# A hybrid decoder step on one Trainium2 core: the new tokens' products in two float32r passes over stacked high and low parts

## The chip, the cores and the metric

The kernel runs on one core of one Trainium2 chip. The metric is device time in microseconds (us) of one execution, as the median of several runs. The engines are named as in the profile: PE (TensorE; PEld is its weight load), DVE (VectorE), ACT (ScalarE), POOL (GpSimd) and SP (SyncE, which here issues the DMAs).

## The reference

Two trunk layers work on 512 prompt tokens and on 8 samples with 8 new tokens each (64 new tokens), 1024 model columns, all in float32. Layer 0 projects the modulated tokens onto queries, keys and values of two head groups and onto an indexer; group A attends to the top-k keys that the indexer selects (128 for a prompt query, 256 for a sample's), group B to all keys with forget gates; the samples also read paged caches. Layer 1 is a chunked gMLP. Each mixer is followed by a convolutional FFN. What matters here is this, with h the modulated tokens of a layer:

```python
hp = xp * (1 + sc1p) + sh1p
hs = xs * (1 + sc1s) + sh1s
...
qa, ka, va, qi, ki, wi, qb, kb, vb, fb = jnp.split(h @ w_in, offs, axis=-1)
...
z = jax.nn.gelu(h @ w_in, approximate=False)
u, v = jnp.split(z, 2, axis=-1)
return u, layer_norm(v, lnv_g, lnv_b)
...
mix_s = (u * mixed) @ w_out_c[j]
xs = layer_norm(ALPHA * xs + (1 + g1s) * mix_s, ln1_g[i], ln1_b[i])
```

The products that the change touches are h @ w for the columns qi, vb (512 columns each), va, ka, qa (512 each) and the gMLP's v (2048), and of these the rows of the 64 new tokens only.

## The kernel before, in words

Activations lie transposed: 8 blocks kb (or k) of 128 model columns on the partitions, 576 tokens along the free axis (512 prompt tokens, then the 64 new ones). To keep float32's precision on PE at the speed of float32r, a value x is split into a high part xh, x rounded to float32r, and a low part xl = x - xh, and so is each weight (wh, wl); a product is then three float32r matmuls, high times high, high times low, low times high. `weights` (L243 to L255) loads a block of 128x1024 raw weights into wr by SP (L250), casts it to wh on ACT (L251) and subtracts to wl on DVE or POOL (L254); wr, wh and wl have three buffers each.

Most products are written with the weights stationary. The products named above are token-major: the tokens are stationary, the weights move, and the result has tokens on the partitions. `token_unit` (L685 to L703) does it for one weight load, a unit: of n = 256 weight columns the load holds four values of k, of n = 512 two. For the four blocks of 128 prompt tokens (tb 0 to 3) it calls `mm3` for each k (L283 to L285, three float32r matmuls). For the 64 new tokens (tb 4) it runs, for each k, one matmul in full float32 (L702): stationary is xn, the unsplit new tokens (128x64), moving the raw weights wr; even k go to the PSUM rows 0 to 63 and odd k to 64 to 127, each on one half of PE's columns. `both_halves` (L715) adds the two halves later, by a copy on ACT (L717) and an add on DVE (L718). The trace shows each of these matmuls as two records, so a unit of n = 256 has eight (x8), one of n = 512 four.

Three places call it. `project` multiplies qi and vb, two blocks of four units with n = 512, from `w_ab` (L836, L868). `project_a` (L920) multiplies va, ka and qa, each in two halves of two units with n = 256, from `w_aa`: 12 units; after each token block its `between` sends out pieces of the samples' attention and of the top-k selection. `gmlp` (L548) multiplies v in eight blocks of two units with n = 256, from `w_v`: 16 units, where `lead` (L573) runs tb 2, 3 and 4 of a unit and the loop below it tb 0 and 1.

The new tokens' xn has two sources. In layer 0 `modulate` (L421 to L431) makes t = x*(1+scale)+shift on DVE for each kb, copies its last 64 columns to xn on POOL (L430), and splits t into xh and xl (`split_to`: ACT copy L760, DVE subtract L761). For later products `Norm.finish` (L117 to L162) makes xn for the whole 1024 columns on DVE and splits it. Four norms exist; three of them have a next product and make xn, and only the one ahead of the gMLP has a reader of it.

The order of the instructions on each engine comes from a scheduler, from the order of the calls, priorities and the buffers that come free, so an edit of one place moves others. The DVE's top-k of the samples (MAX8 and MATCH_REPLACE8 rounds, L1068 and L1069) stands between `project` and the rest of `project_a`; it ends in the selection mask sels (L1187 to L1190). SP's queue holds all loads in order: pages of the caches (L269, tile own), weights (L250) and modulation weights (L372).

Of the kernel before, what the change touches and what calls it, by code (L numbers as in the profile page):

```python
# [10 lines left out]
F32 = mybir.dt.float32  # L11
# [7 lines left out]
P = 128  # L19
D = 1024  # L20
KB = 8
# [38 lines left out]
class Norm:  # L60
# [56 lines left out]
    def finish(self, part):  # L117
# [19 lines left out]
        if part:  # L137
            ps = psum.tile([P, KB, NS], F32, name="tp", bufs=2)
            for kb in range(KB):
                nc.tensor.transpose(ps[:, kb], rt[:NS, 4, kb * P:(kb + 1) * P], ident[:NS, :NS])  # L140
            self.xn = xp.tile([P, KB, NS], F32, name="xn")
            t = self.xn.rearrange("p k (b q) -> p k b q", b=8)
            wide = lambda m: m[:, :, :, None].to_broadcast([P, KB, 8, 8])
            nc.vector.tensor_tensor(t, ps.rearrange("p k (b q) -> p k b q", b=8), wide(self.gains), op=OP.mult)
            nc.scalar.copy(x[:, :, NP:], ps)
            nc.vector.tensor_tensor(t, t, wide(self.offs), op=OP.add)
            net.split_to(*(w[:, :, NP:] for w in self.out), self.xn)
        for k0 in range(0, KB, 2):
# [12 lines left out]
            nc.scalar.copy(h, t)  # L161
            nc.vector.tensor_sub(l, t, h.bitcast(F32))  # L162
# [40 lines left out]
class Net:  # L203
# [217 lines left out]
    def modulate(self, xk, sc1, sh, kb, pool):  # L421
# [7 lines left out]
        nc.vector.tensor_tensor(ts, ts, sh[:, kb, 1:9, None].to_broadcast([P, 8, 8]), op=OP.add)  # L429
        nc.gpsimd.tensor_copy(self.xn[:, kb], t[:, NP:])  # L430
        self.split_to(*(x[:, kb] for x in self.xhl), t)  # L431


# [114 lines left out]
    def gmlp(self, x, last, psum, pool, xp, *norm):  # L548

        nc, a, xs, xn = self.nc, self.a, last.xs, last.xn  # L550
        g1 = self.plus_one(1, 2, xp, "g1")
# [21 lines left out]
        def lead():  # L573
# [4 lines left out]
            units.append(self.weights(a["w_v"][c, u], 1024))  # L578
            self.token_unit({tb: accs[tb // 4][:, tb % 2] for tb in (2, 3, 4)}, units[u], u, 256, xs, xn, True, (2, 3, 4))

# [3 lines left out]
        for c in range(8):  # L584
            first = None
            for u in range(2):
                if c not in led or u == len(led[c][0]):
                    lead()
                units, accs = led[c]
                first = first or psum.tile([P, 2, 256], F32, name="acc", bufs=4)  # L590
                self.token_unit([first[:, 0], first[:, 1]], units[u], u, 256, xs, xn, True, (0, 1))
            accs = [first] + led.pop(c)[1]
# [91 lines left out]

    def token_unit(self, accs, w, u, n, xs, xn, shared=False, tbs=range(5), between=None):  # L685

# [4 lines left out]
        for tb in tbs:  # L691
            for j in range(per):
# [7 lines left out]
                else:  # L700
                    c = 64 * (k % 2)
                    self.nc.tensor.matmul(accs[tb][c:c + NS], xn[:, k], wk[2], start=k < 2, stop=k >= KB - 2,  # L702
                                          tile_position=(0, c))  # L703
            if between:
                between()

    def token_product(self, accs, srcs, xs, xn, n, between=None, shared=False, before=None):

        for u, src in enumerate(srcs):
            w = self.weights(src, 1024)  # L710
            if before:
                before(u)
            self.token_unit(accs, w, u, n, xs, xn, shared, between=between)

# [55 lines left out]
    def project(self, keep, pool, room, psum, free):  # L770
# [5 lines left out]
        xs = self.xs = [self.halves(tuple(x[:, kb] for x in self.xhl)) for kb in range(KB)]  # L776
        self.xn = pool.tile([P, KB, NS], F32, name="xn")
        self.sc1 = pool.tile([P, KB, 9], F32, name="sc1")
# [56 lines left out]
        toks = self.five(psum)  # L835
        self.token_product(toks, [a["w_ab"][0, u] for u in range(4)], xs, self.xn, 512, None, False, before)  # L836
        qit = self.pair(tmp, [P, 4, NP], "qit")
# [5 lines left out]
        kd = tmp.tile([P, 5, P], F32, name="kd")  # L843
        rt = tmp.tile([P, 5, 64], F32, name="rt8")
        for n, t0, t1 in ((P, 0, 4), (NS, 4, 5)):
# [18 lines left out]
        for ci, name in enumerate(("qi", "vb")):  # L864
            accs = toks
            if ci:
                accs = self.five(psum)
                self.token_product(accs, [a["w_ab"][ci, u] for u in range(4)], xs, self.xn, 512, between)  # L868
            for tb in range(5):
# [50 lines left out]
    def project_a(self, pool, psum, xs, between):  # L920
# [3 lines left out]
        for c, name in enumerate(("va", "ka", "qa")):  # L924
            for half in range(2):
                cols = slice(256 * half, 256 * half + 256)
                accs = [psum.tile([P, 2, 256], F32, name="s", bufs=5) for _ in range(3)]
                self.token_product([accs[tb // 2][:, tb % 2] for tb in range(5)], [a["w_aa"][c, half, u] for u in range(2)],
                                   xs, self.xn, 256, between, True)
                for i in range(3):  # L930
# [703 lines left out]
```

## Time and profile before

| what | value |
|---|---|
| median of 3 runs | 1940.66 us (1937.17 to 1941.69) |
| profiled execution | 1944.53 us, of which the span of its instructions is 1942.8 us |
| granted clock of PE, mean | 0.972 |
| PE busy | 1826.5 us, 94% |
| PEld busy | 1622.8 us, 84% |
| DVE busy | 1157.8 us, 60% |
| ACT busy | 743.7 us, 38% |
| POOL busy | 351.3 us, 18% |

The profile is of one execution. Busy is the time in which an engine works on an instruction; PE's matmuls are pipelined, so a matmul's length is longer than the step to the next one's start, and the step is what counts. A granted clock of 1.00 is 2.4 GHz, 0.5 is 1.2 GHz. In a row, `tc<-wr,xn` is the output's name and the inputs' names; `[4.54 <-DVE mx L1332]` is the time in which the engine sat idle before the row, and what ended it.

### The profile page before, as it was taken

Reading aid. Unit: us, or ns where it says so; the run is one execution under the profiler, and the core shown is the slowest. Engines: PE = TensorE matmul, PEld = TensorE weight load, DVE = VectorE, ACT = ScalarE, POOL = GpSimd, SP = SyncE. Lnnn points to the kernel's source line nnn. Section 1 sums busy time; section 2 is a strip of 40 time slices with the busy share of each in tenths; the row PEclk is TensorE's granted clock in tenths of the full one; section 3 lists DMA queues with packets and bytes.
Section 4 is the critical chain, followed back from the end, with each engine's and each line's share of the span. In section 5 each row is a group of like instructions: output and inputs, shape, how many; then the busy total and the mean of one; then the engine's idle time right before and its main releaser. Section 6 shows DMA issues by size and latency. Waiting matters only on the chain. (4 is left out here: it accounts for less than half of the span.)

```text
span 1942.8 us, 37068 instructions
## 1 busy us (share of the span) xinstructions
PE 1826.5 (94%) x14460; PEld 1622.8 (84%) x14460; DVE 1157.8 (60%) x2426; ACT 743.7 (38%) x1382; POOL 351.3 (18%) x518
## 2 busy tenths in 40 slices
PE   6889999899889899999999999999998999999996
PEld 4647877655459799999999989999997999999995
DVE  2549963465448754545556963465577655555577
ACT  2323222255443542424345432422234535344543
POOL 2323511110015310101012330110013101010124
PEclk9989999999899999999999999999998999999997
DMA  8346577797874335353543422332132222213242
GB/s 288 127 155 219 179 253 244 241 307 232 266 240 149 116 131 189 135 161 135 195 141 107 131 92 78 97 97 59 63 112 72 78 97 67 97 56 108 87 139 92
DMA packets 140865, 283.36 MB, mean 146 GB/s; under 512 B 32722, under 2 KB 43922, under 8 KB 140690
## 3 DMA queue, kind: packets, MB, share of 16 engines
q1 hardware_dynamic: 139970, 278.64, 43.9%
q0 software_dynamic: 720, 2.36, 0.5%
q8 instruction: 114, 1.87, 0.4%
q14 instruction: 61, 0.50, 0.1%
HBM read 270.00 MB, written 10.94 MB: 145 GB/s over the span
## 5 line engine op out<-in xcount | busy, mean ns | idle before, releaser
L298 PE MATMUL acc<-xl,wh 128*128 128x256 f32 (+1 forms) x1664 | 496.2, 298 | 5.9 <-DVE xl L162 5.9
L298 PE MATMUL acc<-xh,wh 128*128 128x256 f32 (+1 forms) x1664 | 498.6, 300 | 2.9 <-ACT xh L161 1.7
L298 PE MATMUL acc<-xh,wl 128*128 128x256 f32 (+1 forms) x1664 | 495.0, 298 | 0.0
L251 ACT CAST wh<-wr 128x1024 fp32r<-128x1024 f32 (+2 forms) x276 | 260.7, 949 | 537.3 <-PE acc L298 375.3
L254 DVE TENSOR_TENSOR wl<-wr,wh 128x1024 fp32r<-128x1024 f32 (+2 forms) x211 | 226.7, 1076 | 248.0 <-ACT wh L251 222.4
L298 PEld LDWEIGHTS acc<-xh,wh 128*128 128x128 f32 x1664 | 318.2, 191 | 11.7 <-issue 6.4
L298 PEld LDWEIGHTS acc<-xl,wh 128*128 128x128 f32 x1664 | 318.5, 191 | 7.5 <-DVE xl L162 7.1
L298 PEld LDWEIGHTS acc<-xh,wl 128*128 128x128 f32 x1664 | 318.5, 191 | 0.4 <-issue 0.4
L254 POOL TENSOR_TENSOR wl<-wr,wh 128x1024 fp32r<-128x1024 f32 x65 | 160.9, 2476 | 526.6 <-ACT wh L251 471.8
L298 PE MATMUL acc<-gl,wh 128*128 128x256 f32 (+1 forms) x704 | 209.5, 299 | 0.0
L298 PE MATMUL acc<-gh,wl 128*128 128x256 f32 (+1 forms) x704 | 207.8, 298 | 1.6 <-DVE wl L254 1.6
L298 PE MATMUL acc<-gh,wh 128*128 128x256 f32 (+1 forms) x704 | 208.2, 301 | 0.4 <-ACT gh L760 0.4
L439 DVE SCALAR_TENSOR_TENSOR x<-acc,g,x 128x256 f32<-128x256 f32 x256 | 119.7, 476 | 116.9 <-PE acc L298 111.5
L525 DVE SCALAR_TENSOR_TENSOR y<-up,wc,y 128x592 f32<-128x592 f32 x176 | 150.6, 856 | 34.0 <-ACT y L522 30.0
L298 PEld LDWEIGHTS acc<-gh,wh 128*128 128x128 f32 x704 | 132.9, 190 | 5.5 <-ACT wh L251 2.1
L298 PEld LDWEIGHTS acc<-gh,wl 128*128 128x128 f32 x704 | 132.8, 190 | 2.9 <-DVE wl L254 1.9
L298 PEld LDWEIGHTS acc<-gl,wh 128*128 128x128 f32 x704 | 133.9, 190 | 0.3 <-DVE gl L761 0.2
L518 POOL COPY tail<-up 128x2 f32<-128x2 f32 x88 | 26.3, 299 | 519.1 <-ACT up L516 518.8
L516 ACT COPY up<-acc 128x256 f32<-128x256 f32 x176 | 65.2, 371 | 129.9 <-PE acc L298 121.7
L283 PE MATMUL s<-wh,xh 128*128 128x256 f32 (+1 forms) x256 | 81.7, 327 | 1.4 <-ACT wh L251 1.4
L522 ACT ACTIVATE y<-up,wc 128x592 f32<-128x592 f32 x88 | 77.8, 884 | 9.2 <-POOL up L514 1.1
L285 PE MATMUL s<-wh,xl 128*128 128x256 f32 (+1 forms) x256 | 81.3, 317 | 0.0
(442 smaller groups left out, 3468.3 us busy)
## 6 DMA issues: line engine op xcount, KB each, us to landing
wr<-in_w_up SPq DMA_DIRECT2D x88, 512.0 KB
wr<-in_w_down SPq DMA_DIRECT2D x32, 512.0 KB
wh<-in_w_mod SPq DMA_DIRECT2D x30, 512.0 KB
wl<-in_w_mod SPq DMA_DIRECT2D x30, 512.0 KB
wr<-in_w_mod SPq DMA_DIRECT2D x28, 512.0 KB
own<-in_kT_b SPq DMA_DIRECT2D x48, 256.0 KB
own<-in_v_b SPq DMA_DIRECT2D x44, 256.0 KB
wr<-in_w_down SPq DMA_DIRECT2D x32, 320.0 KB
```

Of the source, the lines that this page charges most:

```text
L251: nc.scalar.copy(h, r)
L254: (nc.vector if low == "v" else nc.gpsimd).tensor_sub(l, r, h.bitcast(F32))
L283: mm(out, sh, mh, start=start, stop=False)
L285: mm(out, sl, mh, start=False, stop=stop)
L298: mm(acc, w[:, k * P:(k + 1) * P], m, start=i == 0, stop=i == n - 1)
L439: nc.vector.scalar_tensor_tensor(xp, acc[:, :256], g1[:, ob, 0:1], xp, op0=OP.mult, op1=OP.add)
L516: nc.scalar.copy(u[:, 2 + 256 * part:258 + 256 * part], accs[part][:, :256])
L518: nc.gpsimd.tensor_copy(tail[:, blk, 0:2], u[:, NP:NP + 2])
L522: nc.scalar.activation(y[:, :n], u[:, 0:n], AF.Identity, bias=wc[:, 3, blk:blk + 1], scale=wc[:, 0, blk:blk + 1])
L525: nc.vector.scalar_tensor_tensor(y[:, :n], u[:, k:k + n], wc[:, k, blk:blk + 1], y[:, :n], op0=OP.mult, op1=OP.add)
```

## The change

The new tokens go over to two float32r passes. A tile xst holds, for each k, the high part and the low part of the 64 new tokens side by side, 128 columns in all. For each k two float32r matmuls (after: L705 to L707) have it as their stationary side, with wh moving and then wl, into the same PSUM tile: its upper 64 rows gather xh times w, its lower 64 rows xl times w, and `both_halves` adds them as before. The 64-column matmuls of full float32 on half of PE's columns are gone: 64 matmuls in the gMLP, 48 in `project_a`, 16 in `project`, and in their place stand 128, 96 and 32.

xst is made by POOL copies behind the split: in `modulate` two of 128x64 for each kb in the place of the one to xn, in `Norm.finish` two of 128x512 behind the split of xn, which is kept. The three norms with a next product each make it. wr is no longer read by PE. The scratch tile of the rope of kd moves from `tmp`'s pool to `pool`'s "rt".

```diff
@@ Norm.finish
             net.split_to(*(w[:, :, NP:] for w in self.out), self.xn)
+            self.xst = xp.tile([P, KB, 2, NS], F32R, name="xst")
+            for i, w in enumerate(self.out):
+                nc.gpsimd.tensor_copy(self.xst[:, :, i], w[:, :, NP:])
@@ modulate
-        nc.gpsimd.tensor_copy(self.xn[:, kb], t[:, NP:])
         self.split_to(*(x[:, kb] for x in self.xhl), t)
+        for i, x in enumerate(self.xhl):
+            nc.gpsimd.tensor_copy(self.xst[:, kb, i], x[:, kb, NP:])
@@ token_unit
-                    c = 64 * (k % 2)
-                    self.nc.tensor.matmul(accs[tb][c:c + NS], xn[:, k], wk[2], start=k < 2, stop=k >= KB - 2,
-                                          tile_position=(0, c))
+                    x = xst[:, k].rearrange("p i n -> p (i n)")
+                    for i in range(2):
+                        self.nc.tensor.matmul(accs[tb], x, wk[i], start=k + i == 0, stop=k + i == KB)
@@ project
-        self.xn = pool.tile([P, KB, NS], F32, name="xn")
+        self.xst = pool.tile([P, KB, 2, NS], F32R, name="xst")
...
-        rt = tmp.tile([P, 5, 64], F32, name="rt8")
+        rt = pool.tile([P, 512], F32, name="rt", bufs=2)[:, :320].rearrange("p (t d) -> p t d", t=5)
```

In the other hunks the argument xn becomes xst.

The order on PE at the norm ahead of the gMLP (tc is the PSUM tile of the new tokens and of the norm's transposes L83, acc that of the prompt tokens). Before:

```order
L283 MATMUL acc<-wh,xh 128x256
L284 MATMUL acc<-wl,xh 128x256
L83 MATMUL tc<-c_ident,x 128x128
L702 MATMUL tc<-wr,xn 64x256 x2
L83 MATMUL tc<-c_ident,x 128x128 x3
L702 MATMUL tc<-wr,xn 64x256 x2
L285 MATMUL acc<-wh,xl 128x256
```

After:

```order
L83 MATMUL tc<-c_ident,x 128x128
L707 MATMUL tc<-wh,xst 128x256
L707 MATMUL tc<-wl,xst 128x256
L707 MATMUL tc<-wh,xst 128x256
L83 MATMUL tc<-c_ident,x 128x128 x3
L707 MATMUL tc<-wl,xst 128x256
L707 MATMUL tc<-wh,xst 128x256
L707 MATMUL tc<-wl,xst 128x256
L707 MATMUL tc<-wh,xst 128x256
L707 MATMUL tc<-wl,xst 128x256
L287 MATMUL acc<-wl,xh 128x256
```

Eight matmuls take the place of four around the same transposes.

The order on POOL at the same norm (L254, after: L257, is the subtract to wl; L168, after: L171, the residual). Before:

```order
L519 COPY tail<-up_8301 128x16
L254 TENSOR_TENSOR wl<-wr,wh 128x1024 x10
L168 TENSOR_SCALAR x<-x,ga,ba 128x576 x8
L607 MEMSET one 128x128
L560 TENSOR_TENSOR ws<-ws,tmp 128x1024
```

After:

```order
L257 TENSOR_TENSOR wl<-wr,wh 128x1024 x8
L150 COPY xst<-xh 128x8x64
L150 COPY xst<-xl 128x8x64
L257 TENSOR_TENSOR wl<-wr,wh 128x1024 x2
L171 TENSOR_SCALAR x<-x,ga,ba 128x576 x8
```

The two copies stand between the eighth and the ninth of ten subtracts.

The order on SP where `project_a`'s weights meet the cache pages (own). Before, the third load of w_aa, some rows later the fourth:

```order
L250 DMA wr<-in_w_aa 128x1024
L903 DMA d_qb<-tmp 128x512
L237 DMA i_c_newm<-in_c_newm 128x256
...
L903 DMA d_qb<-tmp 128x512 x2
L269 ISA
L269 DMA own<-in_kT_b 128x512
...
L250 DMA wr<-in_w_aa 128x1024
L269 ISA
L269 DMA own<-in_kT_b 128x512
```

After, the fourth to sixth:

```order
L272 DMA own<-in_kT_b 128x512
L907 DMA d_qb<-tmp 128x512
L253 DMA wr<-in_w_aa 128x1024 x2
L907 DMA d_qb<-tmp 128x512
L253 DMA wr<-in_w_aa 128x1024
L272 ISA
L272 DMA own<-in_kT_b 128x512
```

The fourth load has moved ahead of four page loads, and two more follow it at once, where before they stood apart among the pages.

## Rows read from the trace of the kernel before

**Rows 1.** The page, busy time of each engine.

```profile
PE 1826.5 (94%) x14460; PEld 1622.8 (84%) x14460; DVE 1157.8 (60%) x2426; ACT 743.7 (38%) x1382; POOL 351.3 (18%) x518
```

**Rows 2.** Windows: length, busy us (instructions) per engine, PEclk, DMA share, GB/s.

```profile
135.00:235.00 100.00, 99.22 (x728) 80.58 (x726) 99.44 (x224) 33.67 (x65) 47.85 (x62) 1.00 0.61 206
235.00:380.00 145.00, 130.36 (x1348) 100.43 (x1348) 75.19 (x173) 33.22 (x67) 26.36 (x19) 0.93 0.74 245
380.00:500.00 120.00, 106.29 (x1030) 65.03 (x1025) 65.92 (x229) 62.24 (x182) 10.14 (x8) 0.94 0.92 275
1155.00:1235.00 80.00, 80.00 (x647) 72.33 (x644) 27.41 (x49) 22.20 (x34) 0.00 (x0) 1.00 0.29 93
```

**Rows 3.** Timeline, PE, one gMLP unit: start us, length us, engine, instruction.

```profile
1161.39 1.08 PE L702 MATMUL tc<-wr,xn 128*64 128x256 f32 x8
1162.40 0.39 PE L283 MATMUL acc<-wh,xh 128*128 128x256 f32 x1
1162.63 0.28 PE L284 MATMUL acc<-wl,xh 128*128 128x256 f32 x1
...
1168.13 0.28 PE L285 MATMUL acc<-wh,xl 128*128 128x256 f32 x1
1168.34 1.08 PE L702 MATMUL tc<-wr,xn 128*64 128x256 f32 x8
```

**Rows 4.** Timeline, PE, the new tokens' products with one block of `w_aa`.

```profile
254.14 1.08 PE L702 MATMUL s<-wr,xn 128*64 128x256 f32 x8
255.15 0.39 PE L283 MATMUL s<-wh,xh 128*128 128x256 f32 x1
255.38 0.28 PE L284 MATMUL s<-wl,xh 128*128 128x256 f32 x1
```

**Rows 5.** Timeline, PE, first projections; in brackets the idle time before.

```profile
34.01 1.94 PE L702 MATMUL s<-wr,xn 128*64 128x512 f32 x8
36.94 0.50 PE L283 MATMUL tp<-xh,cums 128*80 128x256 f32 x2 [0.99 <-ACT xh L760]
...
59.78 0.39 PE L284 MATMUL s<-wl,xh 128*128 128x512 f32 x1
60.02 0.40 PE L285 MATMUL s<-wh,xl 128*128 128x512 f32 x1
60.34 1.08 PE L702 MATMUL s<-wr,xn 128*64 128x512 f32 x4
61.35 0.35 PE L283 MATMUL tp<-xh,cums 128*80 128x256 f32 x1
```

**Rows 6.** Timeline, ACT and PE, end of the sample's top-k.

```profile
242.53 1.06 ACT L1190 ACTIVATE sels<-pS 64x1032 fp32r<-64x1032 f32 x1 [2.92 <-DVE pS L1189]
...
243.42 1.93 PE L1329 MATMUL s<-own,qbdb 128*32 128x256 f32 x16 [4.54 <-DVE mx L1332]
```

**Rows 7.** Groups by shape, POOL: line, shapes, count, busy us, mean ns.

```profile
L168 POOL TENSOR_SCALAR x<-x,ga,ba 128x576 f32<-128x576 f32 x24 | 27.7, 1170 | 43.7 <-DVE tmp L159 43.7
...
L430 POOL COPY xn<-tmp 128x64 f32<-128x64 f32 x8 | 1.8, 238 | 21.2 <-DVE tmp L429 21.2
...
L1451 POOL CAST mtl<-outbl 128x256 fp32r<-128x256 f32 x1 | 0.4, 403 | 0.0
```

**Rows 8.** Timeline, DVE and POOL, ahead of a norm.

```profile
1464.13 0.16 DVE L460 TENSOR_TENSOR rsz<-rsy 128x3 f32<-128x3 f32 x1
1464.32 2.25 DVE L461 TENSOR_TENSOR rsz<-rsz,var 128x3 f32<-128x3 f32 x1
...
1464.12 2.43 POOL L254 TENSOR_TENSOR wl<-wr,wh 128x1024 fp32r<-128x1024 f32 x1 [4.68 <-ACT wh L251]
```

**Rows 9.** Timeline, POOL, ahead of the gMLP's products.

```profile
1114.04 5.20 POOL L254 TENSOR_TENSOR wl<-wr,wh 128x1024 fp32r<-128x1024 f32 x2 [3.27 <-ACT wh L251]
```

**Rows 10.** Waits, whole span: waiter, releaser, us in total, times, longest.

```profile
ACT wh L251 <- DMA wr<-in_w_aa: 32.7, 7, 8.7
...
SPq L250 <- PE tc L702: 91.3, 15, 17.8
```

More of the change, by code (lines that the diff above doesn't have):

```diff
@@ L548, in gmlp @@
     def gmlp(self, x, last, psum, pool, xp, *norm):
-        nc, a, xs, xn = self.nc, self.a, last.xs, last.xn
+        nc, a, xs, xst = self.nc, self.a, last.xs, last.xst
         g1 = self.plus_one(1, 2, xp, "g1")
@@ L578, in lead @@
             units.append(self.weights(a["w_v"][c, u], 1024))
-            self.token_unit({tb: accs[tb // 4][:, tb % 2] for tb in (2, 3, 4)}, units[u], u, 256, xs, xn, True, (2, 3, 4))
+            self.token_unit({tb: accs[tb // 4][:, tb % 2] for tb in (2, 3, 4)}, units[u], u, 256, xs, xst, True, (2, 3, 4))
         for _ in range(3):
@@ L590, in gmlp @@
                 first = first or psum.tile([P, 2, 256], F32, name="acc", bufs=4)
-                self.token_unit([first[:, 0], first[:, 1]], units[u], u, 256, xs, xn, True, (0, 1))
+                self.token_unit([first[:, 0], first[:, 1]], units[u], u, 256, xs, xst, True, (0, 1))
             accs = [first] + led.pop(c)[1]
@@ L683, in rows, with token_unit @@
         return bass.AP(tensor=ap.tensor, offset=ap.offset, ap=[[0, n]] + [list(s) for s in ap.ap[1:]])
-    def token_unit(self, accs, w, u, n, xs, xn, shared=False, tbs=range(5), between=None):
+    def token_unit(self, accs, w, u, n, xs, xst, shared=False, tbs=range(5), between=None):
         per = 1024 // n
@@ L700, in token_unit, with token_product @@
                 else:
-                    c = 64 * (k % 2)
-                    self.nc.tensor.matmul(accs[tb][c:c + NS], xn[:, k], wk[2], start=k < 2, stop=k >= KB - 2,
-                                          tile_position=(0, c))
+                    x = xst[:, k].rearrange("p i n -> p (i n)")
+                    for i in range(2):
+                        self.nc.tensor.matmul(accs[tb], x, wk[i], start=k + i == 0, stop=k + i == KB)
             if between:
                 between()
-    def token_product(self, accs, srcs, xs, xn, n, between=None, shared=False, before=None):
+    def token_product(self, accs, srcs, xs, xst, n, between=None, shared=False, before=None):
         for u, src in enumerate(srcs):
@@ L712, in token_product @@
                 before(u)
-            self.token_unit(accs, w, u, n, xs, xn, shared, between=between)
+            self.token_unit(accs, w, u, n, xs, xst, shared, between=between)
     def both_halves(self, acc, out):
@@ L835, in project @@
         toks = self.five(psum)
-        self.token_product(toks, [a["w_ab"][0, u] for u in range(4)], xs, self.xn, 512, None, False, before)
+        self.token_product(toks, [a["w_ab"][0, u] for u in range(4)], xs, self.xst, 512, None, False, before)
         qit = self.pair(tmp, [P, 4, NP], "qit")
@@ L867, in project @@
                 accs = self.five(psum)
-                self.token_product(accs, [a["w_ab"][ci, u] for u in range(4)], xs, self.xn, 512, between)
+                self.token_product(accs, [a["w_ab"][ci, u] for u in range(4)], xs, self.xst, 512, between)
             for tb in range(5):
@@ L928, in project_a @@
                 self.token_product([accs[tb // 2][:, tb % 2] for tb in range(5)], [a["w_aa"][c, half, u] for u in range(2)],
-                                   xs, self.xn, 256, between, True)
+                                   xs, self.xst, 256, between, True)
                 for i in range(3):
```

## The prediction

> **What bounds the kernel now.** I read the page's busy times first, then the windows by stage, then TensorE's timeline where the changed matmuls stand, and last the waits. PE is busy 1826.5 of 1942.8 us, 94% of the span [rows 1], so any time taken out of PE's stream counts, where that stream is what the stage waits for. The windows say where this is so [rows 2]. In 1155 to 1235 us, which holds most of the gMLP's v product, PE is busy 80.00 of 80.00 us: what is cut there comes out of the total whole. In 135 to 235 us DVE is busy 99.44 of 100 us with the top-k, so that stage keeps its length, and what is saved ahead of it counts only if the top-k starts sooner. In 235 to 380 us, where project_a runs between pieces of attention, PE is busy 130.36 of 145 us and the DMA engines 0.74: mostly PE, with gaps. In 380 to 500 us DMA is at 0.92, so a gain made ahead of it can be lost there again, if the cache pages don't come sooner too.
>
> The changed matmuls stand in three of these places: 8 units with n = 512 in the first projections (two blocks of four weight loads), 12 units with n = 256 in project_a (three outputs, two halves, two loads), and 16 units with n = 256 in the gMLP (eight blocks, two loads). An n = 256 unit takes 4 values of k from a weight load, an n = 512 unit 2.
>
> **The gMLP, part by part.** The trace gives one unit in full [rows 3]: the eight records of the new tokens begin at 1161.39 and the next unit's at 1168.34, a period of 6.95 us. From the second float32r matmul behind them (1162.63) to the 48th (1168.13) there are 46 steps in 5.50 us, 0.1196 us each. The 48 token-block matmuls at that pace would take 5.74 us, so the new tokens' group costs 6.95 - 5.74 = 1.21 us: 1.01 us from its first record to the next block's first matmul, and some 0.10 us more on either side (that first matmul is followed after 0.23 us, and the group starts 0.21 us behind the matmul before it, where 0.12 is the pace). After the change the group is 4 x 2 = 8 float32r matmuls of 128x256 with a full 128-column stationary side, the same form as their neighbours: 8 x 0.1196 = 0.96 us, with no other tile shape among them. A unit falls to 56 x 0.1196 = 6.70 us and saves 0.25 us. Twelve of the 16 units lie in the gapless stretch: 12 x 0.25 = 3.0 us. The other four stand at the norm ahead, where the order cuts the groups up and mixes them with transposes and token-block matmuls, and PE also waits; I count them at 0.7 us of at most 1.0. Together **-3.7 us**.
>
> How far the pass count alone carries this: the row shows 1.01 us for 4 values of k in full float32, and 0.96 us is forecast in two float32r passes, so of the 0.25 us a unit 0.05 lies in the work and 0.20 in the steps around the switched group. The Trainium skill ("FP8 and Floating Point Precision", TensorE Precision Notes) says that a true FP32 matmul is four passes through the array; with two 64-column tiles at work side by side that is the work of two passes for each k, the same as after the change, and by that rule alone the sum would be nothing.
>
> **project_a.** The group there has the same steps [rows 4]: from 254.14 to the next matmul at 255.15, 1.01 us, and 0.23 us from that one to the next. So 0.25 us a unit again. The first of the 12 units runs ahead of a gap in which PE sits for 4.54 us until DVE gets to it [rows 6], so its gain is lost; 11 x 0.25 = 2.75 us is the most that stream time gives. The least is nothing, if the DMA-bound stretch behind takes it all. With PE at 90% here I take **-2.0 us**.
>
> **The first projections.** A group of an n = 512 unit lasts from 60.34 to 61.35, 1.01 us, and starts 0.32 us after the matmul before it, where 0.24 is the pace (59.78 to 60.02) [rows 5]. Four float32r matmuls at 0.24 take 0.96 us, so a unit in a full stream gives back about 0.15 to 0.25 us, and 8 of them 2 us at most. Against this, the old group needed only the landed weights and xn, so two units (eight records) ran at 34.01 to 35.95, ahead of an idle stretch that ended at 36.94 on ACT's xh [rows 5]. Now they need wh, wl and xst, which come after that same wait; their 2 x 0.96 = 1.9 us go into the stream behind. A wait for wl can add one POOL subtract, 2.43 us [rows 8]. Everything here reaches the end only through the start of the top-k, which ends in the sample's sels at 242.53 [rows 6]. The ends are -2.0 us and +1.9 + 2.4 = +4.3 us; I take **0**, since the gain and the move are of the same size, and the wait for wl is one that the token blocks of the unit had before.
>
> **The copies into xst.** In modulate 8 copies of 64 columns, 0.238 us each [rows 7], become 16: +1.9 us of POOL in a stretch where the engine has idle time, hidden there. In Norm.finish six copies of 8 x 64 = 512 columns are new, two in each of three norms. No row shows this shape; 128x256 takes 0.403 us and a 128x576 scale 1.170 us [rows 7]. The nearest by operation is the copy, so I take twice that, 0.8 us; the six are 4.8 us of POOL. Ahead of the gMLP POOL is idle for 3.27 us until 1114.04 [rows 9], so that pair costs nothing if it falls there; the order puts it just behind eight subtracts and ahead of the last two. In the other two norms the tile is never read, but while POOL works, DVE may stand: at 1464.32 an operation that otherwise takes 0.16 us takes 2.25, beside a POOL subtract of 2.43 us from 1464.12 [rows 8]. If each pair holds the norm's DVE chain whole, that is 2 x 1.6 = 3.2 us; with none held, 0. By the upper price it is 4 x 1.17 = 4.7 us. I take **+1.0 us**, one of the two pairs partly in the way.
>
> **The weights.** wr is free once wh and wl are made, not once PE has read it. SyncE's queue waits 91.3 us in all for the old matmuls [rows 10]; those waits go, and the order has the fourth to sixth loads of w_aa several page loads sooner. What is late next is the same buffers' wl, or DMA itself. In the gMLP nothing waits for weights in the full stretch, so it is worth 0 there; in project_a the waits of ACT for a w_aa load add up to 32.7 us in 7 [rows 10], most of it ACT being early. I take 0 here and keep the gain as a rival. The kd rope's scratch tile comes from another pool of the same size class; 0.
>
> Sum: -3.7 - 2.0 + 0 + 1.0 = **-4.7 us**. The profiled execution took 1944.53 us, of which the span is 1942.8; it becomes 1939.8. It lies 3.9 us above the median of the runs, 1940.66, so against that median the forecast is **1936.0 us**. About 0.2%, 3.9 us, is what a measurement of this kernel can tell from no change; the forecast lies only just beyond.
>
> **The rivals.**
> (a) *No gain*: the group costs as much in two passes as before, because the steps around it stay (0.20 of the 0.25 us a unit). Then the gMLP and project_a give 27 x 0.05 = 1.4 us, the copies take 1.0 back: 1940 us. For it: nothing in the trace shows this very group in float32r. Against it: token-block matmuls follow each other at 0.1196 us also where the stationary side and the bank change. By the rule on passes above, the time would be this one. Chance 0.10.
> (b) *The gMLP alone*: project_a's gain is absorbed by the DMA-bound attention at 0.92 [rows 2]. -3.7 + 1.0: 1938.0 us, called the same. Chance 0.22.
> (c) *More*: the earlier w_aa loads also take waits out of project_a's 14.6 idle PE us [rows 2]; if a third of them goes, 5 us more, 1931 us. Chance 0.13.
> (d) *Slower*: the top-k starts late. The place is the first projections: the new tokens' matmuls now queue on PE behind wl and xst, and everything behind them on PE, the indexer's queries among it, waits with them; the top-k's 100 us of full DVE pass any delay on to 242.53. The price is the 1.9 us of the two moved units, and a POOL subtract of 2.43 us for each unit of the first block that has to wait for its low part. From a delay of 4.7 us on (two such waits) the kernel is slower than now; with four it is 1.9 + 9.7 = 11.6 us, and the time 1936.0 + 11.6 = 1947.6 us. For it: these units ran ahead of the high parts in an idle slot. Against: within a unit the token blocks come first and need wl themselves, so the new tokens seldom wait anew. Chance 0.12. A pair of copies that locks DVE is in the sum already; the Trainium skill ("SBUF — State Buffer", Who interferes with whom) gives the reason for that lock, one port pair that VectorE and GpSimd hold in turn, and the 2.25 us row agrees.
>
> **How the numbers follow.** The forecast's own case has 0.43; its spread is about 3 us either way, 1933 to 1939. With (c), faster by over 0.2% (under 1936.8) is 0.13 + 0.43, less a quarter of the latter on the slow side, plus a quarter of (b), whose time lies 1.2 us from the bound: 0.51. Slower by over 0.2% (above 1944.5) is most of (d): 0.10. The rest, 0.39, is within. The range runs from 1930, past (c), to 1943, some 2 us beyond no gain at all and one wait of (d); more than that is left out.
>
> **What would show it.** Right: the gMLP period falls from 6.95 to about 6.70 us; the changed group's eight matmuls step by 0.12; SyncE's waits for the tc tile are gone; the attention ends some 2 us sooner. Wrong: the period stays at 6.9 or more (a); sels ends later than 242.5 by over 2 us (d), or sooner by as much, which no term here gives; the stretch from 235 to 560 us changes by more than 3 us (c); a norm's DVE chain shows an operation stretched by the new copies beyond 1 us each.

## The result, and the profile after

The changed kernel took 1930.11 us (median of 6 runs, 1929.12 to 1932.75) where the kernel before took 1939.49 us beside it (6 runs, 1936.87 to 1941.69): a ratio of 0.9949, 95% interval 0.9935 to 0.9963, 9.4 us less. A second set of runs, in the experiments below, gave 0.9924 (0.9904 to 0.9944), 1927.46 against 1942.09 us. The forecast was 4.7 us less, and its time, 1936.0, was 6 us too high; the measured time lies at the fast end of the range (1930 to 1943).

The page of the changed kernel, busy time of each engine: PE's is 9.3 us less than in [rows 1].

```profile
PE 1817.2 (94%) x14460; PEld 1639.1 (85%) x14460; DVE 1154.3 (60%) x2426; ACT 744.2 (39%) x1382; POOL 367.7 (19%) x532
```

The window that answers to the second line of [rows 2], with the same columns:

```profile
235.00:380.00 145.00, 134.28 (x1396) 110.16 (x1396) 81.95 (x199) 34.94 (x72) 30.57 (x30) 0.93 0.81 264
```

The stretch of project_a is denser: from 235 to 380 us PE is idle for 10.7 us instead of 14.6, and the DMA engines are at 0.81 instead of 0.74. To see what each stage gave, the stages have to be cut at the same work, not at the same time.

The gMLP's units on PE's timeline, one group of the new tokens, and the start of the next:

```profile
1168.29 0.28 PE L288 MATMUL acc<-wh,xl 128*128 128x256 f32 x1
1168.41 0.28 PE L707 MATMUL tc<-wh,xst 128*128 128x256 f32 x1
...
1169.25 0.28 PE L707 MATMUL tc<-wl,xst 128*128 128x256 f32 x1
1169.37 0.28 PE L286 MATMUL acc<-wh,xh 128*128 128x256 f32 x1
...
1175.13 0.28 PE L707 MATMUL tc<-wh,xst 128*128 128x256 f32 x1
```

Eight matmuls take 0.96 us (1168.41 to 1169.37) with no longer step on either side, and the period is 1175.13 - 1168.41 = 6.72 us, where it was 6.95 [rows 3].

But at the head of the gMLP waits are new. PE's timeline there, in brackets the idle time before a row:

```profile
1120.75 0.39 PE L286 MATMUL acc<-wh,xh 128*128 128x256 f32 x1 [0.73 <-ACT xh L164]
...
1122.91 0.39 PE L288 MATMUL acc<-wh,xl 128*128 128x256 f32 x1 [1.42 <-DVE xl L165]
```

The units that PE works on while the norm is split end sooner, and PE then stands for the split, 2.2 us in these two rows. Before, PE's one wait here was for the norm's x, 2.1 us just ahead of the gMLP, and that one is still there.

The stages of two profiles of each kernel (the second one of before and the second one of the change are experiments below). sels is the end of the mask sels on ACT, project_a the stretch from there to the last qbda copy on POOL, the attention's end the last low part of the mixed heads (mtl on DVE):

| us | before | before, 2nd | after | after, 2nd |
|---|---|---|---|---|
| start to sels | 243.6 | 243.7 | 250.1 | 243.1 |
| project_a | 131.9 | 130.5 | 122.8 | 122.8 |
| project_a's end to the attention's end | 202.4 | 202.8 | 193.1 | 198.8 |
| to the first xn of a norm (output product) | 52.4 | 52.2 | 50.6 | 50.7 |
| FFN of layer 0, to the next xn | 476.4 | 476.8 | 477.8 | 477.6 |
| norm, to the gMLP's first new-token matmul | 15.1 | 15.1 | 14.9 | 14.9 |
| gMLP, to the third xn | 352.8 | 352.8 | 350.1 | 350.1 |
| last FFN and norm | 468.2 | 468.2 | 468.7 | 468.6 |
| span | 1942.8 | 1942.1 | 1928.1 | 1926.6 |

By the means of the two profiles the spans differ by 15.1 us: +3.0 up to sels, -15.1 from there to the attention's end, -1.7 in the output product, +1.1 in the FFN, -0.2 and -2.7 in the gMLP's norm and the gMLP, +0.5 behind. The 15.1 us are more than the 9.4 of the first set of runs and near the 14.6 of the second, so the stages tell where the gain lies better than how large it is. Nearly all of it came from layer 0, in the stretch from sels to the end of attention, where the forecast had -2.0. That one stretch in the windows, of before and of after:

```profile
243.60:577.90 334.30, 295.55 (x2945) 199.79 (x2940) 170.69 (x513) 132.54 (x351) 41.93 (x31) 0.93 0.81 254
```

```profile
250.10:566.00 315.90, 287.55 (x2944) 201.32 (x2936) 169.36 (x513) 133.60 (x352) 42.08 (x31) 0.95 0.84 265
```

As many matmul records, but for one, take 8.0 us less of busy PE (one part is the matmuls themselves, another the granted clock, 0.95 after 0.93), and PE is idle for 315.90 - 287.55 = 28.4 us instead of 38.8. In the second profiles PE idles there for 36.3 and 28.5 us.

What stood in the way before is seen around the ninth unit of project_a. ACT, POOL, DVE and PE in the kernel before, in brackets the idle time and what ended it:

```profile
318.38 1.05 ACT L251 CAST wh<-wr 128x1024 fp32r<-128x1024 f32 x1 [5.84 <-DMA wr<-in_w_aa]
319.33 0.58 ACT L937 COPY tmp<-s 128x512 f32<-128x512 f32 x1
...
319.50 2.38 POOL L254 TENSOR_TENSOR wl<-wr,wh 128x1024 fp32r<-128x1024 f32 x1 [12.24 <-ACT wh L251]
...
319.95 2.49 DVE L725 TENSOR_TENSOR ro<-tmp,i_c_cos 128x512 f32<-128x512 f32 x1 [5.29 <-ACT tmp L937]
...
325.50 0.45 PE L741 MATMUL tp<-c_ident,ro 64*128 64x64 f32 x2 [3.73 <-DVE ro L728]
```

ACT works in order. It sits at the cast of the next weights until their load lands at 318.38, and the copy of a finished product (L937) is queued behind that cast; DVE's rope waits 5.29 us for this copy, and PE 3.73 us for the rope. The late cast costs twice: POOL's subtract, released by it, runs beside the rope's first operation, which takes 2.49 us there and took 0.69 at 312.57.

Of ACT's seven waits for a load in this stage, this is the one that cost PE more than 0.5 us. In project_a PE was idle for 10.1 us (131.90 - 121.81) before and for 6.2 (122.80 - 116.61) after; before, 3.7 of it is this wait, and of the others the larger ones, at the end of the stage, are there after too, each changed by under 1 us. The second profile of before has the wait again, 3.15 us. And at this place the granted clock fell. The stretch around the wait, and 100 us of project_a before and after:

```profile
324.00:331.00 7.00, 5.50 (x34) 3.76 (x34) 1.74 (x6) 1.59 (x3) 2.36 (x1) 0.52 0.78 237
```

```profile
260.00:360.00 100.00, 95.68 (x1036) 75.80 (x1036) 43.12 (x98) 21.55 (x44) 19.82 (x12) 0.97 0.72 239
```

```profile
260.00:360.00 100.00, 99.78 (x1123) 86.45 (x1122) 48.64 (x115) 25.76 (x53) 20.00 (x12) 1.00 0.77 255
```

PE sat idle until 325.50 and was granted close to 1.2 GHz from 324 to 331 us; after the change it has neither the wait nor the slow stretch.

In the changed kernel the loads come earlier. The load for the cast in the next row was issued at 295.22, 25 us ahead of it, where the one that landed at 318.38 in the kernel before was issued at 312.04. The cast waits only until the last reader of a wh buffer is done:

```profile
320.58 1.05 ACT L254 CAST wh<-wr 128x1024 fp32r<-128x1024 f32 x1 [1.01 <-PE s L707]
```

SyncE's waits for the tc tile and ACT's waits for a load of w_aa [rows 10] are gone. In their place stands this shorter one, from the waits of ACT:

```profile
ACT wh L254 <- PE s L707: 11.5, 7, 3.0
```

### The profile page after: what moved, and what is told of

The parts are those of the page before. It is cut to its first block, busy times and chain, and to the rows that moved or that the text cites. A ratio compares the mean times of both kernels' runs of the same rounds, so it can differ in the third digit from the quotient of the medians.

```text
span 1928.1 us, 37084 instructions
## 1 busy us (share of the span) xinstructions
PE 1817.2 (94%) x14460; PEld 1639.1 (85%) x14460; DVE 1154.3 (60%) x2426; ACT 744.2 (39%) x1382; POOL 367.7 (19%) x532
## 5 line engine op out<-in xcount | busy, mean ns | idle before, releaser
L254 ACT CAST wh<-wr 128x1024 fp32r<-128x1024 f32 (+2 forms) x276 | 260.8, 949 | 520.4 <-PE acc L301 374.8
L257 DVE TENSOR_TENSOR wl<-wr,wh 128x1024 fp32r<-128x1024 f32 (+2 forms) x211 | 225.7, 1071 | 248.0 <-ACT wh L254 221.9
L257 POOL TENSOR_TENSOR wl<-wr,wh 128x1024 fp32r<-128x1024 f32 x65 | 160.5, 2470 | 503.6 <-ACT wh L254 488.0
L287 PE MATMUL s<-wl,xh 128*128 128x256 f32 (+1 forms) x256 | 81.7, 319 | 0.2 <-POOL wl L257 0.2
```

The costliest lines, as they stand in the source:

```text
L254: nc.scalar.copy(h, r)
L257: (nc.vector if low == "v" else nc.gpsimd).tensor_sub(l, r, h.bitcast(F32))
L287: mm(out, sh, ml, start=False, stop=False)
```

## The experiments

The theory after the result was *early weights*: the two passes free the raw tile wr before PE comes to the unit's end, SyncE loads w_aa sooner, and ACT no longer holds up the chain of copy, rope and transposes. The rivals were *stream* (only the shorter groups count, 0.25 us a unit), *order* (the scheduler gave the attention a better order by chance) and *late front* (what the first projections lose is lost at the end). All ratios are to the kernel before on the same chip. The runs of one build spread over 3.5 to 17 us, so the stages of the profiles tell more than the times. But a profile is one execution, and where the granted clock falls differs between two executions of one build: the attention of the changed kernel took 193.1 and 198.8 us with PE idle for 22.2 and 22.3 us and the same order of work on PE, at a granted clock of 0.94 and 0.92.

### One place at a time

gmlp_only: the two passes in the gMLP alone; all norms make xst, as in the change. The line by which the gMLP takes it:

```diff
-        nc, a, xs, xn = self.nc, self.a, last.xs, last.xn
+        nc, a, xs, xn = self.nc, self.a, last.xs, last.xst
```

> Only the gMLP has the two float32r passes; both products of layer 0 stay in full float32 on the raw weights. The stream theory: 16 units by 0.25 us at most, so 3 to 4 us under the kernel before, about 1936, with a unit's period of 6.70 us in the gMLP and layer 0 as before. The rival that the period hardly falls: within 1 us of before. The theory that most of the gain comes from layer 0 needs this run to stay above 1935.

Ratio 0.9973 (0.9960 to 0.9986), 5 us. Its profile gives the gMLP 351.6 us against 352.8, so of the 5 us only 1.2 are in the stage that was changed; layer 0 ended at the same time as before (attention's end at 578.3), and the last FFN was 3.2 us shorter, which other builds with an unchanged gMLP show too (before_ev below: 465.4). The period was 6.7 us as in the changed kernel; the rest was lost at the gMLP's head, which took 33.8 us up to its first gap-free unit instead of 32.6. There the changed kernel took 32.2 us at a granted clock of 1.00, gmlp_only 33.8 at 0.95.

layer0_only: the change without its part in the gMLP and the norms.

> Only layer 0 has the two passes; the gMLP multiplies xn in full float32 as before, and the norms make no xst. Early weights theory (ACT's casts of w_aa no longer wait for their loads, so the chain from ACT to PE in project_a gets shorter): 5 to 7 us under before, about 1933, the last q output of project_a some 4 us earlier although sels is later. Stream theory: 11 units by 0.25 us, less what the later sels costs: within 3 us of before. The sum of this gain and that of the gMLP alone should be the 9.4 us of the whole change if nothing else is at work.

Ratio 0.9923 (0.9906 to 0.9940), 1929.33 against 1943.32 us. project_a took 124.1 us, sels to the attention's end 320.4. That is more than either theory had, and layer 0 alone gives as much as the whole change, within what runs can tell; the gains of the parts don't add up to the tenth of a per cent.

proja_only: the two passes in project_a alone, with xst made from the split in that stage.

```diff
+        self.xst = self.own.tile([P, KB, 2, NS], F32R, name="xst")
+        for i, x in enumerate(self.xhl):
+            nc.gpsimd.tensor_copy(self.xst[:, :, i], x[:, :, NP:])
```

> Only project_a has the two passes; the first projections and the gMLP stay in full float32. xst is made for it in its own stage by two copies of 512 columns. Early weights theory: the gain of layer 0 without the later sels of the changed kernel (sels was 6.5 us later there): 6 to 12 us under before, about 1931, sels at 242 to 243 us. If the later sels costs nothing at the end, the same 5 to 7 us as with all of layer 0. Stream theory: 2 to 3 us.

Ratio 0.9992 (0.9979 to 1.0005): no gain in the runs, a miss for both theories. The stage itself did what was expected: sels at 244.0, project_a 121.9 us instead of 131. The attention behind it took 202.4 us, as before, and ended at 568.3 instead of 577.9; the output product gave 3.5 us back (55.9). Its profiled span was 1936.8 us, 5 to 6 us less than those of before. Why its other runs don't show this is open.

best1: this with the gMLP's part, and xst in one norm.

> Two passes in project_a and in the gMLP, full float32 on the raw weights in the first projections, and xst made only in the one norm that is read. By both gains (project_a alone 6 to 9, gMLP 3): 1927 to 1930, somewhat under the changed kernel. If the later start of the top-k costs the changed kernel its 6.5 us whole: 1924.

Ratio 0.9971 (0.9958 to 0.9983). project_a 121.7 us, sels 244.4, the attention's end 566.9, the gMLP 351.6. It was expected to beat the changed kernel and does not.

proj_only: the two passes in the first projections alone. project_a's new tokens are there xh + xl, put together by one POOL add.

> The first projections alone in two passes; project_a (whose new tokens are put together again as xh + xl by one POOL add) and the gMLP in full float32. Theory of a late front: sels 3 to 6 us later than the 243.7 of the kernel before, project_a's end later by as much, since the stretch between stays at 131 us, and the whole 1 to 6 us over before. Rival: the late sels is made up in project_a and the attention, and the time is that of before within 2 us.

Ratio 0.9987 (0.9974 to 1.0000). sels at 246.0, project_a 129.6, the attention's end at 576.9: the front comes later by 2.4 us and the end of attention is where it was, so this run bears out the rival that a delay of this size is made up behind it.

### Holding the raw weights, or freeing them

after_hold: the changed kernel with one small matmul per unit of project_a that reads wr.

```diff
+                        if hold and i and j == per - 1:
+                            self.nc.tensor.matmul(accs[tb][0:16, 0:4], self.cs[:, 0, 16:32], w[2][:, 0:4], start=False, stop=False)
                         self.nc.tensor.matmul(accs[tb], x, wk[i], start=k + i == 0, stop=k + i == KB)
```

> The changed kernel, and in project_a each unit has one more small float32 matmul (16 zero columns by 4 columns of the raw weights, added into the new tokens' sum) just ahead of its last float32r matmul, so that the raw weights stay in use until then, as before the change; SyncE's order of the w_aa loads is that of the kernel before again. The 12 matmuls cost some 12 x 0.2 us at most of themselves. Early weights theory: the waits of ACT for w_aa come back (some 30 us in 7), and the time rises by 4 to 8 us, to 1934 to 1938. Stream theory: at most 2.5 us, 1930 to 1932.5.

Ratio 1.0030 (1.0015 to 1.0046): the whole gain is gone and more, which is beyond both theories. ACT's waits for w_aa are back, 30.8 us in 9, and from sels to the attention's end it looks like the kernel before (PE idle 328.40 - 289.28 = 39.1 us, clock 0.93):

```profile
246.90:575.30 328.40, 289.28 (x2967) 203.13 (x2962) 173.50 (x513) 132.62 (x352) 44.20 (x33) 0.93 0.83 264
```

But project_a grew only from 122.8 to 126.4, and the small matmuls have a price of their own (0.58 us from the matmul ahead of it to the second one behind it, where two steps take 0.24: some 0.34 us each, 4.1 us for 12). So a pair was made in which only the operand differs, on the kernel with project_a alone: proja_small_wh reads wh, which the unit holds anyway, proja_small_wr reads wr. The line of the first and that of the second:

```diff
-    self.nc.tensor.matmul(accs[tb][0:16, 0:4], self.cs[:, 0, 16:32], w[0].bitcast(F32)[:, 0:4], start=False, stop=False)
+    self.nc.tensor.matmul(accs[tb][0:16, 0:4], self.cs[:, 0, 16:32], w[2][:, 0:4], start=False, stop=False)
```

> project_a alone in two passes, and in each of its 12 units one more small float32 matmul (16 zero columns by 4 columns of wh, added into the new tokens' sum). It reads wh, which the unit uses anyway, so it holds nothing longer; by the rows of the earlier kernel with such matmuls one costs 0.34 us, 12 of them 4.1 us. Both theories: the stretch from sels to project_a's end 4 us longer than the 121.9 us of project_a alone, about 126, and ACT never waits for a load of w_aa.

> The same with the raw weights in the small matmul's place: nothing else differs, but the raw tile is held until the unit's end, and SyncE's order of the loads is that of the kernel before. Early weights theory: ACT waits some 30 us for w_aa again and the stretch from sels to project_a's end is 4 to 6 us longer than with wh, about 131, that of the kernel before. Theory that only the matmuls themselves count: the same 126 us as with wh, within 1.5 us, though ACT waits.

The stretch from sels to the attention's end, with wh and with wr:

```profile
242.70:559.50 316.80, 290.48 (x2949) 203.67 (x2945) 170.27 (x510) 131.86 (x350) 38.93 (x28) 0.95 0.82 261
```

```profile
243.20:566.30 323.10, 285.38 (x2955) 201.72 (x2954) 169.40 (x510) 131.84 (x351) 42.57 (x31) 0.95 0.84 263
```

With wr ACT waits for the loads again:

```profile
ACT wh L251 <- DMA wr<-in_w_aa: 27.9, 8, 9.3
```

project_a took 124.6 us with wh and 130.0 with wr, 5.4 us more, which is the amount that early weights had; to the attention's end the difference is 6.3 us, with PE idle for 26.3 and 37.7 us. But the chain is another one. No wait of ACT for a load cost PE more than 0.8 us here; 3.1 of the 5.4 us are the last rope of project_a, for which PE waits 5.46 us with wr and 2.41 with wh, and which itself waited 5.66 us for a store (d_qa<-ro). The runs don't tell the two apart: 0.9948 (0.9932 to 0.9964) and 0.9946 (0.9930 to 0.9962). And both are faster than proja_only, by half a per cent, with 12 matmuls more: the attention took 192.2 and 193.1 us there instead of 202.4. The code behind project_a is the same, but PE's order of work there is another in each of the three. With wh PE idles 20.5 us in the attention instead of 27.0; with wr it idles 27.7 us, but is granted 0.96 of its clock instead of 0.93.

The other way round, before_wr4 lets the next raw weights come sooner without touching a matmul: by a fourth wr buffer. Room for it comes from two scratch tiles moved, and before_ev has that move alone.

```diff
-WB = (3,3,3)
+WB = (4,3,3)
```

> The kernel before with two scratch tiles of the first projections moved to buffers of another pool (the rope's scratch as in the change, and the small products' row tile), which makes the room that the next kernel needs. No theory gives it a gain: within 2 us of before. If it is faster by 4 us or more, the gain of the change is a matter of how the scheduler happens to order the work.

> The kernel before with the same two tiles moved and a fourth buffer for the raw weights; every matmul is as before. SyncE can issue each load of w_aa about one unit sooner. Early weights theory: most of layer 0's gain comes without any change of the matmuls, 4 to 7 us under before, about 1934. Stream theory: no gain, within 1.5 us of before.

before_ev has 0.9978 (0.9964 to 0.9993), 4 us that no theory gave it, and by the mark set ahead this speaks for the order as a part of the gain: project_a took 131.0 us, the attention 199.9, and the last FFN 465.4. before_wr4 has 1.0006 (0.9990 to 1.0023), project_a 124.6 us, 6.4 less, and no wait of ACT for w_aa over 1.4 us. The stretch from sels to the attention's end, without and with the fourth buffer:

```profile
241.80:572.70 330.90, 297.77 (x2945) 202.45 (x2939) 171.95 (x514) 133.13 (x351) 41.62 (x31) 0.93 0.81 256
```

```profile
251.10:574.40 323.30, 290.54 (x2942) 198.41 (x2934) 174.19 (x519) 132.28 (x350) 39.85 (x30) 0.94 0.83 265
```

So early loads alone make most of project_a's gain. In this build PE's wait at the ninth unit is 1.15 us, where before_ev has 3.62. But it starts its sels 9 us later, and nothing is left of the gain: in the time, a miss for early weights. A second profile of each:

> The kernel before with a fourth raw buffer, a second profile. The first had sels at 251.1 us, 9 us later than without the buffer, and a shorter stretch from sels to the end of attention (323.3 against 330.9 us). If the late front belongs to the build, sels is at 249 to 252 again; if it was one run's, at 242 to 245, with the end of attention at 565 to 570 instead of 574.4. The stretch itself should be 320 to 326 us again if the early loads shorten it.

> Its pair without the fourth buffer, a second profile: sels at 241 to 245, the stretch to the end of attention 329 to 334 us, PE idle in it 33 to 39 us.

sels came at 253.9 us again, project_a took 123.6, the attention ended at 581.6; without the buffer 244.3, 131.8 and 571.9. So the late front belongs to the build with the buffer, and the shorter project_a too (8.2 us less this time). The stretch to the attention's end does not: 327.7 us with the buffer, outside the 320 to 326 expected, and 327.6 without. The attention took 204.1 and 195.8 us, with PE idle for 29.8 and 23.7. Early loads alone don't shorten the attention.

### The second profiles, another order, the unread copies

> The kernel before, profiled a second time. Its first profile was 5 us over the median of its runs. If that excess lies in the DMA-bound attention, the stretch from the last q output of project_a (367.6 us) to the start of layer 0's output product should be shorter here by up to 5 us and all else the same; if it lies elsewhere, the times of sels (242.5) or of project_a's end differ.

The second profile of before agrees with the first to 1.4 us in every stage of the table, and its execution took 1943.84 us, on a chip where the median of before was 1943.32. So the first profile had no excess in any one stage.

> The changed kernel again, beside the three others on one chip and with a second profile. 7 to 12 us under before. Its attention stage (project_a's end to the last of the mixed heads) took 193.1 us where the kernel before takes 202.4 and 202.8; the theory that this is the scheduler's order, which is the same in every run of one build, needs 193 to 196 again; if it was an accident of one run, about 200.

The second profile of the change had sels at 243.1 us, 7 us earlier than the first; the rows of the two, first and second:

```profile
249.04 1.06 ACT L1194 ACTIVATE sels<-pS 64x1032 fp32r<-64x1032 f32 x1 [2.92 <-DVE pS L1193]
```

```profile
242.07 1.06 ACT L1194 ACTIVATE sels<-pS 64x1032 fp32r<-64x1032 f32 x1 [2.92 <-DVE pS L1193]
```

project_a took 122.8 us both times, and the attention ended at 566.0 and at 564.7. So of 7 us of a late sels 1.3 were left at the end of attention; the attention took 193.1 and 198.8 us, between the two cases of the expectation. Nothing that waits made this up: PE idled as long in both, and the first execution, with the late sels, had the better clock in the attention.

after_ev: the changed kernel with one scratch tile moved, which gives another order in layer 0, the attention's among it.

```diff
-        raw = tmp.tile([P, 5, 80], F32, name="ev8")
+        raw = pool.tile([P, T], F32, name="tmp", bufs=3)[:, :400].rearrange("p (t d) -> p t d", t=5)
```

> The changed kernel with the small products' row tile of the first projections moved to another buffer, which changes no matmul and only gives the scheduler another order, in the attention too. Theory that the gain is made by the earlier release of the raw weights: PE's idle time from sels to the end of attention stays at 26 to 35 us (37.8 on average where the raw tile is held), and the time 0.4 to 0.8% under before. Theory that it is luck of one order: idle back at 36 to 40 us and at most 0.3% under.

Ratio 0.9930 (0.9905 to 0.9955). project_a 122.9 us, and in the stretch PE is idle for 319.50 - 288.47 = 31.0 us:

```profile
245.40:564.90 319.50, 288.47 (x2944) 202.66 (x2936) 170.72 (x514) 133.59 (x351) 42.05 (x31) 0.94 0.83 261
```

The gain is not that of one lucky order. before_ev has both scratch tiles where after_ev has them, so this pair is the change with the tiles held equal: 0.9930 against 0.9978, each to the kernel before on its own chip, which makes about 0.5%, and project_a takes 122.9 us against 131.0 and 131.8.

after_nodead: the changed kernel with xst in the one norm that is read.

```diff
+            if self.nxt == (1, 0):
```

> The changed kernel without the four copies into the xst tiles that nothing reads (those of the two norms ahead of the FFNs). Theory that they lock DVE in the norms: 1 to 3 us under the changed kernel. Theory that they fall into waits: the same within 1 us, 0.5 to 0.75% under before.

Ratio 0.9915 (0.9893 to 0.9938), 1926.18 us. The stage in which two of the unread copies ran, the FFN of layer 0, took 477.8 us as with them. The last FFN and its norm, where the other two ran, took 466.3 us instead of 468.7, within the spread of that stage over all builds (464.4 to 469.1). So no cost of them shows. It is the smallest ratio, but its interval overlaps that of the changed kernel's second set.

## Why the prediction was wrong

The sign was right, the gain was twice the forecast, and the sum was right for none of its parts. Of its signs, the gMLP's period, the step of 0.12 us and the end of SyncE's waits came as forecast; the attention ended 12 us sooner, not 2; the sign of (c) came in both profiles, and that of (d), a late sels, in one of two.

**The step that failed: the weights, 0.** "in project_a the waits of ACT for a w_aa load add up to 32.7 us in 7 [rows 10], most of it ACT being early. I take 0 here". Most of it was indeed ACT being early: of the seven waits five cost PE nothing and one 0.5 us. One was on the path. Behind its cast stood the copy of a finished product that DVE's rope and PE's transposes wait for, and PE stood for 3.7 us (3.15 in the second profile), though ACT is 38% busy. It came with a second price that the sum doesn't have: the granted clock fell there.

project_a took 122.8 us where it took 131.2 (mean of two). Of these 8.4 us, PE's idle time gives 3.4 (from 9.6 on average to 6.2). PE's busy time gives the other 5.0 (121.6 to 116.6): the shorter groups 2.75 of it, by the prediction's own 0.25 us for 11 units, which leaves some 2.3 us for the clock. This split is an estimate. So the stream term, -2.0, was near, and the term put at 0 was some 5.7 us.

That earlier loads do this is shown best by the fourth buffer, which touches no matmul: project_a took 6.4 and 8.2 us less in its two profiles. The wait at the ninth unit, over 3 us, stands in all six profiles of kernels that read wr in project_a by the old matmuls and have three buffers; each shows a fall of the clock within 3 us of it, and one behind the 1.15 us wait of before_wr4 is the only other in the middle of project_a. The small matmuls that hold wr are weaker evidence: in the pair the 5.4 us lie mostly at another wait, and in the changed kernel project_a grew by 3.6 us, no more than the twelve matmuls themselves cost (4.1): ACT's waits were back, but PE's wait at the ninth unit was 0.54 us. Over all builds that let the weights come early project_a took 121.7 to 124.6 us, over the others 126.4 to 131.9. Rival (c) named the mechanism, with 5 us of idle PE and a chance of 0.13.

**The gMLP, -3.7.** The mechanism was right and the period nearly so (6.72 us for 6.70). From the first gap-free unit to the last the groups took 73.9 us instead of 76.5, -2.6. The four units at the norm were sized wrongly: they were to give -0.7. The head took 32.2 us instead of 32.6, but 33.8 and 33.7 in gmlp_only and best1; behind the last group 0.3 us came on. The better head of the changed kernel goes with the granted clock, which was 1.00 there and 0.95 in the kernel before and in those two builds. after_hold, with the same gMLP, had 33.8 us at 0.95, so the better head is luck and no merit of the new groups. The prediction saw that PE waits there, but not that a shorter filler leaves PE standing for the norm's split.

**The rule on passes, and rival (a).** The steps around the group of 64-column tiles went with it, as the rows said; the Trainium skill ("FP8 and Floating Point Precision", TensorE Precision Notes) counts only passes, which gives nothing, and the period fell by 0.23 us. Most of the cost was at the switch, 0.18 of the 0.23 us.

**Behind project_a, nothing forecast.** Rival (b) let the DMA-bound attention swallow the gain. Instead the attention's end came 12 us earlier: over the two profiles the attention itself was 9.3 and 4.0 us shorter. PE's idle time in it fell from 28.7 and 27.2 us to 22.2 and 22.3, and what the two profiles differ by is the granted clock. Why the idle time fell stays open. Early loads alone don't do it (26.5 and 29.8 us with the fourth buffer), and two moved scratch tiles alone nearly do (24.7 and 23.7 us in before_ev), which points to the order of the work.

So the whole time does not follow the weights alone. With early weights the ratios run from 0.9915 to 1.0006: proja_only and the fourth buffer gain nothing that shows, and proja_small_wr, which holds wr, gains as much as its pair. What is shown is project_a's part.

**The first projections, 0.** Over seven profiles with two passes there sels ends at 246.4 us on average (243.1 to 250.1), over nine without them (the fourth buffer left out) at 243.6: +2.8 us, within the bounds of -2.0 and +4.3. What a late sels costs at the end is open. proj_only's 2.4 us were gone at the end of attention; in the two profiles of the change 7 us shrank to 1.3, by the clock; and in the build with the fourth buffer a sels 9 us late used up all that project_a gained. Rival (d) did not come about in the times, but its mechanism is not refuted.

**The copies, +1.0.** They cost nothing that shows. The two that are read, ahead of the gMLP, are in every such run; that norm took 14.9 us instead of 15.1.

## What to carry to other kernels

A wait for a load on an engine that works in order can cost what is queued behind it, however idle the engine is. The sum of such waits tells little, since here one of seven made up nearly all that counted: before they are priced at nothing, look for the instruction that stands next in the queue behind each, and who waits for that. Dropping a buffer's last, slow reader can be worth more than the reader's own time where the buffer's next load is late. Work that fills an engine's wait for another chain saves little when it gets shorter. And where two profiles of one build differ in a stage, compare idle time and granted clock before a cause is named.

## What the runs showed of the hardware

A switch of PE's tile shape showed its cost on both sides of the group: 0.21 us instead of 0.12 from the last 128-column matmul to the first 64-column one, and 0.23 us behind the first matmul after it. A small matmul of 16 columns put among others cost about 0.34 us in its neighbours' pace. The granted clock of PE fell at or just behind its waits of over 3 us in the middle of project_a, in six profiles of six (0.52 over 324 to 331 us in the kernel before), and in the profiles where PE waited there for less than 1 us it stayed at 1.00. An operation of DVE that took 0.69 us at 312.57 took 2.49 at 319.95, beside a POOL subtract. The last FFN and its norm, the same work in every build but for two unread copies, took 464.4 to 469.1 us; what decides it is open. Runs of one build on one chip spread by up to 17 us (1933.23 to 1950.56 for the fourth buffer), far more than the kernel's first three runs had shown.
